# Hybrid trunk on one core: attention between projections, two convolution tiles by stacked taps on TensorE, the scan's carried part at full width

## The chip, the core and the metric

The kernel is one launch on one NeuronCore of a Trainium2 chip. The metric is the device time of a launch in microseconds (us), given as a median over runs. The core has four compute engines that work side by side, each through its own list of instructions in a fixed order: TensorE (PE: matmuls and transposes), VectorE (DVE: elementwise work), ScalarE (ACT: functions, copies) and GpSimd (POOL). SyncE (SP) issues the DMA transfers. The operands lie in SBUF (128 partitions); TensorE writes its sums to PSUM, which has 8 banks of 128 x 512 fp32. An engine that reaches an instruction whose inputs or whose buffer are not ready waits there, and all that stands behind it on that engine waits too.

## What is computed

Two layers over 576 tokens (512 of a prompt, 64 of eight samples with state). Layer 0 is a Conformer convolution (width 31, 512 channels) and sliding-window attention side by side, then a convolutional FFN; layer 1 is a Mamba-2 (SSD) mixer, then another FFN. The parts of the reference that the change touches:

```python
# layer 0, mixer
a_val, a_gate, q, k, v = split(h @ w_in)
u = a_val * sigmoid(a_gate)
padded = concatenate([conv_hist, u])                 # 30 rows of history ahead
c = silu(layernorm(causal_dwconv(padded, conv_w, conv_b)))   # 31 taps a channel
q, k = rope(rmsnorm(q)), rope(rmsnorm(k))
o = sink_attention(q, k, v, ...)                     # 8 heads, blocks of 128 queries, 256 keys
out = concatenate([c, o]) @ w_out

# layer 1, chunks of L = 128 tokens
w_intra = (cb[..., None] * decay * dtc[:, :, None])
y_diag = einsum('bclsgr,bcsgrp->bclgrp', w_intra, xc)
h_prev = ...                                         # state carried into each chunk
y_off = einsum('bclgn,bcgrpn,bclgr->bclgrp', cc, h_prev, exp(acum))
y = y_diag + y_off
```

## The kernel before

**Projections.** Everything lies with channels on the partitions and the 576 tokens along the free axis, in two halves of 288. Each projection takes weight tiles of 512 KB (`wr`, three buffers, loaded through SP's queue), splits them into a high part on ACT (`wh`, L148) and a low part on DVE (`wl`, L149), and does three matmuls a tile of 128 channels (`mm3`, L158 to L160: high x high, high x low, low x high). `units` runs a list of such projections, each with a function that empties its PSUM sums. `out_proj` adds the sums to the residual `x` on DVE (L257).

**Buffers and order.** SBUF is cut into slots; `S(name)` takes the slot that has been free longest, `free` gives it back, and whoever takes a slot waits for its last users. PSUM banks are dealt out in rings by name (`self.rings`): in this stage `mm` has banks 0 and 1, `sc` (attention scores) 4 to 6, `pt` (transposes) 7 and 2, `po` (attention sums) 3. A scheduler that runs at build time puts each engine's instructions into a fixed order from the program text, the dependencies and its own estimates.

**mix0.** The convolution input `u` of tile i (4 tiles of 128 channels) is written to `cap[i]` (prompt, 30 columns of history ahead) and `cas_v[i]` (samples) by the `val` units. The gate and value units of tiles 0 and 2 come first, then q, k and v, then tiles 1 and 3. The outputs `ca[i]` of the convolution take their slots at the start, with the gates. Tiles 0, 2 and 3 are convolved on DVE: ACT copies `cap` into overlapping segments (`seg`, L397), then one multiply (L686) and 30 multiply-adds (L688) run over 128 x 576. Tile 1 (`PC`) is convolved on TensorE (`pe_conv`): for each of the 31 taps ACT builds three diagonal matrices (L522 twice, L528), and TensorE does three float32r matmuls over 512 prompt columns (L524 to L526) and one fp32 matmul over 64 sample columns (L529). The pieces of `pe_conv` stand in the program between the four attention blocks, which come after all projections but `val` 1 and 3. Per block: scores (L581), softmax (maximum on DVE L553, exponential on ACT L560, scaling on DVE L564), transposes (L596) with a copy by ACT (L598), and the sums with the values (L601). The sample attention (L638 to L660) follows. After this come the layer norm of the convolution (`pm`, L696, needs all four `ca`) and two output projections of 192 matmuls each: of the attention (`oh`, `ol`), then of the convolution (`ch`, `cl`).

**The scan in mix1.** For each of 4 groups of 8 heads, `decays(r)` loads a row of cumulated decays broadcast to 128 partitions (`acb`, L955), makes the decay matrix of a head in `ew` (Relu L960 four times, Exp L961, product L962), and for chunks 1 to 3 scales C by the decay from the chunk's start (Exp L963, product L964). `outputs(t, pair)` takes two heads: 8 matmuls of the inner part (L979) and 6 of the carried part (L977, state times the scaled C) fill one bank `yp`, each with 64 columns of weights; L981 adds it to the skip term. There are 16 such blocks, which stand between the projection matmuls of the following group.

Of the kernel before, what the change touches and what calls it, by code (L numbers as in the profile page):

```python
# [6 lines left out]
F32 = mybir.dt.float32  # L7
# [18 lines left out]
for _name, _w in (  # L26
# [3 lines left out]
    ("cc_w", 24 * 4), ("cc_b", 24), ("dsk", 16), ("gn", 16),  # L30
# [8 lines left out]
for _name, _w in (  # L39
    ("ident", 128), ("prot", 128), ("blk2", 2), ("amask", 256), ("smask", 2 * 192),  # L40
    ("tri", 128), ("tris", 64), ("bmat", 64), ("bsel", 8), ("selx", 256), ("selm", 128),
    ("sel3", 192), ("bsel3", 4),
):
    CV[_name] = _n
    _n += _w
# [3 lines left out]
class Builder:  # L49
    NSLOT = 50  # L50
    EXTRA = 8
# [298 lines left out]
    def mix0(self):  # L350
# [49 lines left out]
        def a_val(i):  # L400
            def go(half, p):
# [3 lines left out]
                else:  # L405
# [89 lines left out]
        for i in (0, 2):  # L495
            sg[i], cap[i], ca[i] = self.S("sg"), self.S("cap", 542), self.S("ca")
# [6 lines left out]
        self.units([gate_unit(2), val_unit(2)] + qkv, 1)  # L503
        self.free(kg, ksq, krs, vf, cos, sin)
        for i in (1, 3):
            sg[i], cap[i], ca[i] = self.S("sg"), self.S("cap", 542), self.S("ca")
        self.units([gate_unit(1), gate_unit(3)], 1)

        self.rings = {"mm": [0, 1], "aux": [4, 5, 6, 7], "sc": [4, 5, 6], "pt": [7, 2], "po": [3]}
        pconv = {}  # L510

        def pe_conv(k0, k1):

            i = PC
            if not pconv:
                pconv[0] = self.pm(), self.pm()
            pp, ps = pconv[0]
            for k in range(k0, k1):
                dg = []
                for w in (cwh, cwl):  # L520
                    dg.append(self.segp.tile([P, P], F32R, tag="dg", bufs=4, name="dg"))
                    nc.scalar.activation(dg[-1], self.ident, AF.Copy, scale=w.bitcast(F32)[:, k:k + 1])  # L522
                sl = slice(k, k + NP)
                nc.tensor.matmul(pp, dg[0], cph[0][:, sl], start=k == 0, stop=False)  # L524
                nc.tensor.matmul(pp, dg[0], cph[1][:, sl], start=False, stop=False)
                nc.tensor.matmul(pp, dg[1], cph[0][:, sl], start=False, stop=k == 30)  # L526
                df = self.segp.tile([P, P], F32, tag="df", bufs=2, name="df")
                nc.scalar.activation(df, self.ident, AF.Copy, scale=self.pv("ca_w", i * 31 + k))  # L528
                nc.tensor.matmul(bt(ps[:, 0:64]), df, cas_v[i][:, :, k:k + 8], start=k == 0, stop=k == 30)  # L529
# [13 lines left out]
        of = [self.S("of") for _ in range(4)]  # L543
# [41 lines left out]
        def values(n, probs):  # L585
# [20 lines left out]
            self.free(held)  # L606
            for j in range(4):
                nc.scalar.activation(of[j][:, n * P:(n + 1) * P], po[:, j * P:(j + 1) * P], AF.Copy)

        ready = []  # L610
        for n in range(4):
            ready.append((n, scores(n)))
            if n == 0:
                self.units([val_unit(1), val_unit(3)], 1)
                self.norm_end()
            else:
                pe_conv((n - 1) * 31 // 4, n * 31 // 4)
            if len(ready) > 1:
                values(*ready.pop(0))
        pe_conv(3 * 31 // 4, 31)  # L620
# [651 lines left out]
```

## Time and profile before

| what | value |
|---|---|
| time, median of 3 runs | 1611.56 us (1610.28 to 1612.52) |
| the profiled execution's own time | 1613.28 us |
| its span (first to last instruction) | 1611.5 us |
| mean granted TensorE clock | 0.994 |
| TensorE busy | 1580.2 us, 98% of the span |
| DVE, ACT, POOL busy | 64%, 43%, 7% |
| first matmul of the `oh` projection | 187.70 us |
| first matmul of FFN 0 | 245.09 us |

How to read the lines that follow: a group's row gives line, engine, operation, tiles as output<-inputs, sizes, the count, then busy time in us, mean ns of one, and how long the engine sat idle ahead of them and for whom. A fp32 matmul shows as two records. The ends of matmuls are modelled, so where the pace matters the starts are compared. A row of the timeline gives the start, the time from the first start to the last end, and the count. A row of windows gives for each engine its busy time and, in brackets, how many instructions began; `PEclk` is the granted clock as a share of the full one.

### The profile page before, as it was taken

The numbers are of one execution on the slowest core, as the hardware profiler recorded it, in microseconds if no ns is written. First come the engines' busy times: TensorE is split into PE (matmuls) and PEld (weight loads), VectorE is DVE, ScalarE is ACT, GpSimd is POOL, SyncE is SP. The second block draws the span as 40 slices with busy tenths as digits, with TensorE's granted clock in tenths as the row PEclk, the third lists the DMA queues.
The fourth block names the chain that finished last, engine by engine and source line by source line (L and its number), as shares of the span: only waits on it lengthen the run. The fifth ranks groups of instructions, "written<-read, shape, count | busy, mean of one in ns | idle before, by whom it ended". The sixth has DMA issues, their size and how long they took to land.

```text
span 1611.5 us, 28699 instructions
## 1 busy us (share of the span) xinstructions
PE 1580.2 (98%) x11704; PEld 1502.4 (93%) x11704; DVE 1024.4 (64%) x1817; ACT 696.1 (43%) x1323; POOL 110.3 (7%) x322
## 2 busy tenths in 40 slices
PE   8999999999999999999999999999899999999999
PEld 8996899999999999998987997998799999999999
DVE  7898777664465364678795676676776653564552
ACT  7248853231222122478764656557452221221220
POOL 0000001000000000111202101101111000000000
PEclk9998999999999999999999999999999999999999
DMA  7222022222222222225235225224222222222222
GB/s 229 71 60 69 14 79 92 91 79 80 91 78 81 93 76 77 74 81 163 96 102 183 80 76 164 97 89 153 98 74 86 91 79 81 91 71 87 92 82 75
DMA packets 63632, 150.05 MB, mean 93 GB/s; under 512 B 18558, under 2 KB 19582, under 8 KB 63502
## 3 DMA queue, kind: packets, MB, share of 16 engines
q1 hardware_dynamic: 63502, 148.23, 29.6%
q8 instruction: 92, 1.51, 0.4%
q14 instruction: 38, 0.31, 0.1%
HBM read 133.86 MB, written 14.34 MB: 92 GB/s over the span
## 4 chain that ended last, share of the span: by engine, by line
PE 88%; DVE 5%; ACT 4%; DMA 3%; issue 1%; POOL 0%; SPq 0%; ACTq 0%; DVEq 0%; POOLq 0%
PE mm L158 26%; PE mm L160 25%; PE mm L159 25%; DMA acb<-acd 2%; PE yp L979 1%; DVE cconv L739 1%; PE pst L928 1%; PE pt L180 1%; ACT wh L148 1%; PE yp L977 1%; PE mm L524 1%; PE pyo L992 1%; PE pr L191 1%; PE pt L915 1%; PE mm L526 1%
## 5 line engine op out<-in xcount | busy, mean ns | idle before, releaser
L158 PE MATMUL mm<-hh,wh 128*128 128x288 f32 (+1 forms) x2288 | 681.0, 298 | 8.5 <-ACT wh L148 7.8
L160 PE MATMUL mm<-hh,wl 128*128 128x288 f32 x2288 | 679.6, 297 | 0.0
L159 PE MATMUL mm<-hl,wh 128*128 128x288 f32 (+1 forms) x2288 | 677.7, 296 | 0.0
L148 ACT ACTIVATE wh<-wr 128x1024 fp32r<-128x1024 f32 (+1 forms) x215 | 223.5, 1039 | 544.9 <-issue 284.8
L158 PEld LDWEIGHTS mm<-hh,wh 128*128 128x128 f32 (+1 forms) x2288 | 429.8, 188 | 14.7 <-ACT wh L148 8.0
L160 PEld LDWEIGHTS mm<-hh,wl 128*128 128x128 f32 x2288 | 429.6, 188 | 4.6 <-issue 2.8
L159 PEld LDWEIGHTS mm<-hl,wh 128*128 128x128 f32 (+1 forms) x2288 | 430.4, 188 | 3.5 <-issue 1.4
L149 DVE TENSOR_TENSOR wl<-wr,wh 128x1024 fp32r<-128x1024 f32 (+1 forms) x215 | 257.6, 1198 | 78.1 <-ACT wh L148 77.9
L158 PE MATMUL mm<-yh,wh 128*128 128x288 f32 x960 | 287.0, 300 | 3.6 <-ACT yh L168 2.5
L159 PE MATMUL mm<-yl,wh 128*128 128x288 f32 x960 | 287.5, 300 | 0.2 <-DVE yl L169 0.2
L160 PE MATMUL mm<-yh,wl 128*128 128x288 f32 x960 | 285.7, 298 | 0.0
L158 PEld LDWEIGHTS mm<-yh,wh 128*128 128x128 f32 x960 | 181.8, 190 | 8.4 <-issue 3.4
L159 PEld LDWEIGHTS mm<-yl,wh 128*128 128x128 f32 x960 | 182.0, 190 | 4.6 <-issue 3.2
L257 DVE TENSOR_TENSOR x<-x,mm 128x288 f32<-128x288 f32 x192 | 85.7, 452 | 155.7 <-PE mm L160 155.4
L160 PEld LDWEIGHTS mm<-yh,wl 128*128 128x128 f32 x960 | 181.8, 189 | 2.9 <-issue 2.8
L302 DVE TENSOR_TENSOR gbuf<-mm,rs 128x224 f32<-128x224 f32 x44 | 17.2, 392 | 107.7 <-PE mm L160 107.7
L313 ACT ACTIVATE gsilu<-gconv,par 128x512 f32<-128x512 f32 x44 | 31.9, 725 | 115.1 <-DVE gconv L310 115.0
L310 DVE SCALAR_TENSOR_TENSOR gconv<-gbuf,par,gconv 128x592 f32<-128x592 f32 x88 | 73.2, 832 | 1.5
L323 DVE TENSOR_TENSOR gsilu<-mm,gsilu 128x288 f32<-128x288 f32 x88 | 40.1, 455 | 49.9 <-PE mm L160 49.9
L688 DVE SCALAR_TENSOR_TENSOR ca<-seg,par,ca 128x576 f32<-128x576 f32 x90 | 71.3, 814 | 0.6
L739 DVE SCALAR_TENSOR_TENSOR cconv<-cbuf,par,cconv 128x600 f32<-128x600 f32 x72 | 61.5, 857 | 11.4 <-ACT cconv L737 10.3
L960 ACT ACTIVATE ew<-acb,ac 128x128 f32<-128x128 f32 x128 | 41.2, 391 | 45.2 <-DMA acb<-acd 34.5
(315 smaller groups left out, 1721.1 us busy)
## 6 DMA issues: line engine op xcount, KB each, us to landing
wr<-in_w_gate SPq DMA_DIRECT2D x44, 512.0 KB, 3.3
wr<-in_w_up SPq DMA_DIRECT2D x44, 512.0 KB, 3.4
wr<-in_w_in_o SPq DMA_DIRECT2D x40, 512.0 KB, 3.5
wr<-in_w_down SPq DMA_DIRECT2D x32, 448.0 KB, 3.4
wr<-in_w_down SPq DMA_DIRECT2D x16, 512.0 KB, 3.5
acb<-acd SPq DMA_DIRECT2D x32, 256.0 KB, 3.6
h<-in_h SPq DMA_DIRECT2D x32, 256.0 KB, 3.0
out_ssm_s<-h SPq DMA_DIRECT2D x32, 256.0 KB, 3.1
```

The source lines that it names most:

```text
L148: nc.scalar.activation(hi[:, :n], raw[:, :n], AF.Copy)
L149: nc.vector.tensor_tensor(lo[:, :n], raw[:, :n], hi[:, :n].bitcast(F32), op=SUB)
L158: nc.tensor.matmul(out, hi[:, ws], xh[:, sl], start=i == 0, stop=False)
L159: nc.tensor.matmul(out, hi[:, ws], xl[:, sl], start=False, stop=False)
L160: nc.tensor.matmul(out, lo[:, ws], xh[:, sl], start=False, stop=i == n - 1)
L257: nc.vector.tensor_tensor(self.x[m][:, sl], self.x[m][:, sl], p[:, :HB], op=ADD)
L310: nc.vector.scalar_tensor_tensor(cv[:, :592], g[:, k:592 + k], w(k), cv[:, :592], op0=MUL, op1=ADD)
L313: nc.scalar.activation(sl[:, :NP], cv[:, :NP], AF.Silu, bias=b)
L323: nc.vector.tensor_tensor(sl[:, HALF[half]], p[:, :HB], sl[:, HALF[half]], op=MUL)
L688: nc.vector.scalar_tensor_tensor(a, sv[:, :, k:k + 8], w, a, op0=MUL, op1=ADD)
L739: nc.vector.scalar_tensor_tensor(cv[:, :600], g[:, k:600 + k], w(k), cv[:, :600], op0=MUL, op1=ADD)
L960: nc.scalar.activation(ew[:, cs], acb[:, cs], AF.Relu, bias=ac[:, o:o + 1], scale=-1.0)
```

## The change

1. **Order in mix0.** The four blocks of attention now stand between the remaining projections: q, k, v directly after tile 0; then scores 0, gate and value 2, scores 1, values 0, gate and value 1, scores 2, values 1, gate and value 3, scores 3, values 2, the sample scores, tile 1's convolution, values 3, the sample values, tile 3's convolution.
2. **Two convolution tiles on TensorE, four taps at a time.** Tiles 1 and 3 (`PC = (1, 3)`) go through a copy in DRAM (`cad`), from which 32 transfers a tile read 32 channels each, shifted by 0 to 3 columns, so that the 128 rows hold 32 channels x 4 taps (`xp4` prompt, `xs4` samples). A weight of 128 x 32 (`w4`, built on POOL) then does four taps at once for 32 channels, in fp32: 8 steps x 4 column groups for the prompt (L536) and as many for the samples (L543). The diagonal matrices on ACT and the split of `cap` go. `ca[i]` takes its slot only when a tile is convolved. DVE keeps tiles 0 and 2.
3. **The carried part of the scan at full width.** `carried(t)` does state times unscaled C for two heads at once, one 128 x 128 x 128 matmul a chunk (L1014, three a block), and scales the product on DVE by `ea2`, the decays of both heads (two loads of 64 x 384, one Exp). `outputs` keeps the 8 matmuls of the inner part (L1027), adds the carried part in a separate DVE instruction, and `ew` is made in place in `acb`.

Lines move by some numbers: L158 to L160 become L160 to L162, L688 becomes L730, L564 L585, L581 L602, L596 L617, L601 L622, L696 L738.

On VectorE, before, the convolution's multiply-adds (L688) stand among the evacuations of the projections (`sg`, `cap`, `kg`) from early in mix0 on:

```order
L686 TENSOR_SCALAR ca<-seg,par 128x576
L382 TENSOR_TENSOR sg<-sg,rs 128x288
L380 TENSOR_TENSOR sg<-mm,rs 128x288
L688 SCALAR_TENSOR_TENSOR ca<-seg,par,ca 128x576
L382 TENSOR_TENSOR sg<-sg,rs 128x288
L149 TENSOR_TENSOR wl<-wr,wh 128x1024
L404 TENSOR_TENSOR cap<-mm,sg 128x288
L688 SCALAR_TENSOR_TENSOR ca<-seg,par,ca 128x576 x3
```

On VectorE, now, at the end of the attention (L585 is the last scaling of the sample softmax, L547 and L548 empty the banks of a convolution tile from TensorE, L171 splits the attention's output):

```order
L585 TENSOR_SCALAR sm<-sm,den 128x192 x2
L728 TENSOR_SCALAR ca<-seg,par 128x576
L730 SCALAR_TENSOR_TENSOR ca<-seg,par,ca 128x576
L547 TENSOR_SCALAR ca<-mm,par 128x512
L730 SCALAR_TENSOR_TENSOR ca<-seg,par,ca 128x576
L548 TENSOR_SCALAR ca<-mm,par 128x64
L730 SCALAR_TENSOR_TENSOR ca<-seg,par,ca 128x576
L728 TENSOR_SCALAR ca<-seg,par 128x576
L730 SCALAR_TENSOR_TENSOR ca<-seg,par,ca 128x576 x8
L171 TENSOR_TENSOR ol<-of,oh 128x576 x4
L730 SCALAR_TENSOR_TENSOR ca<-seg,par,ca 128x576 x35
L547 TENSOR_SCALAR ca<-mm,par 128x512
```

All 62 convolution instructions of tiles 0 and 2 (before: 93 of three tiles, spread over the stage) now stand behind the last softmax. The slot of tile 0's `ca` is one that tile 1's `xp4` gives back, so the first of them also waits for tile 1's matmuls; 14 more, with five additions to `x` (L259) between them, stand behind the rows shown.

On SyncE, before, behind the last value unit (`kct` and `vc` are the sample caches):

```order
L408 DMA out_ca_p<-cap 128x30
L409 DMA out_ca_s<-cas 1024x1x30
L284 DMA fhist<-in_ffn_hist 128x352
L626 DMA kct<-in_kct 128x512
L627 DMA vc<-in_vc 128x512
```

On SyncE, now, at the same place (`cad` is the copy in DRAM; the first two rows are the last of tile 1's 32 loads, which alternate in this way):

```order
L527 DMA xp_1320<-cad_203 32x536
L528 DMA xs_1322<-cad_203 32x8x32
L410 DMA out_ca_p<-cap 128x30
L411 DMA out_ca_s<-cas 1024x1x30
L414 DMA cad_204<-cap 128x542
L415 DMA cad_204<-cas 128x304
L640 DMA kct<-in_kct 128x512
L641 DMA vc<-in_vc 128x512
```

The sample caches now stand behind 32 small loads, which stand behind the last of the four weight tiles of the attention's output projection; another 32 loads for tile 3 follow the caches, ahead of the weights of the convolution's output projection.

On TensorE, one block of the scan before (`hst` is the carried state), and one now:

```order
L979 MATMUL yp<-ew,xdt 64x128 x4
L977 MATMUL yp<-acb,hst 64x128 x2
L979 MATMUL yp<-ew,xdt 64x128 x2
L977 MATMUL yp<-acb,hst 64x128 x2
L979 MATMUL yp<-ew,xdt 64x128 x2
L977 MATMUL yp<-acb,hst 64x128 x2
```

```order
L1014 MATMUL py<-cfm,hst 128x128 x3
L1027 MATMUL yp<-acb,xdt 64x128 x8
```

Fourteen matmuls of 64 weight columns became eight of 64 and three of 128; in most blocks projection matmuls stand between the two rows.

The diff, cut to its core:

```diff
-    NSLOT = 50
-    EXTRA = 8
+    NSLOT = 48
+    EXTRA = 10
...
                 if half == 0:
+                    sg[i], cap[i] = self.S("sg"), self.S("cap", 542)
...
-        PC = 1
-        cph = self.S("cph", 542, F32R), self.S("cpl", 542, F32R)
-        cwh, cwl = (self.segp.tile([P, 31], F32R, name=n_) for n_ in ("cwh", "cwl"))
-        self.split(self.pv("ca_w", PC * 31, 31), (cwh, cwl), slice(0, 31))
+        PC = (1, 3)
+
+        cad = {i: self.dp.tile([P, 846], F32, name=f"cad{i}") for i in PC}
...
-                    if i == PC:
-                        self.split(cap[i], cph, slice(0, 542))
+                    if i in PC:
+                        nc.sync.dma_start(cad[i][:, 0:542], cap[i])
+                        nc.sync.dma_start(cad[i][:, 542:846].rearrange("p (b c) -> p b c", c=38), cas_v[i])
                     else:
                         segment(i)
+                    self.free(cap.pop(i))
...
-        for i in (0, 2):
-            sg[i], cap[i], ca[i] = self.S("sg"), self.S("cap", 542), self.S("ca")
...
-        self.units([gate_unit(2), val_unit(2)] + qkv, 1)
+        self.units(qkv, 1)
...
+        def pe_conv(i):
+            xp4 = [self.S("xp4", 540) for _ in range(4)]
+            xsp = [self.S("xs4", 576) for _ in range(2)]
...
+            for c in range(4):
+                for j in range(4):
+                    n = 540 if j < 3 else 536
+                    m = 36 if j < 3 else 32
+                    r, rc = slice(j * 32, j * 32 + 32), slice(c * 32, c * 32 + 32)
+                    nc.sync.dma_start(xp4[c][r, 0:n], src[rc, j:j + n])
+                    nc.sync.dma_start(xs4[c][r, :, 0:m],
+                                      src[rc, 542:846].rearrange("p (b t) -> p b t", t=38)[:, :, j:j + m])
+            yield
+            pp, ps = self.pm(), self.pm()
+            for s in range(8):
+                k = slice(0, P if s < 7 else 96)
+                for c in (3, 2, 1, 0):
+                    w = w4[i][k, (s * 4 + c) * 32:(s * 4 + c) * 32 + 32]
+                    m = nc.tensor.matmul(pp[c * 32:c * 32 + 32, :], w, xp4[c][k, 4 * s:4 * s + NP], start=s == 0, stop=s == 7)
...
+            ca[i] = self.S("ca")
+            nc.vector.tensor_scalar(ca[i][:, :NP], pp, self.pv("ca_b", i), None, op0=ADD)
+            nc.vector.tensor_scalar(ca[i][:, NP:], ps[:, 0:64], self.pv("ca_b", i), None, op0=ADD)
+            self.free(xp4, xsp)
+            yield
...
+        p0 = scores(0)
+        self.units([gate_unit(2), val_unit(2)], 1)
+        p1 = scores(1)
+        values(0, p0)
+        self.units([gate_unit(1), val_unit(1)], 1)
+        p2 = scores(2)
+        values(1, p1)
+        convs = [pe_conv(i) for i in PC]
+        next(convs[0])
+        self.units([gate_unit(3), val_unit(3)], 1)
+        self.norm_end()
+        p3 = scores(3)
+        sample_loads()
+        next(convs[1])
+        values(2, p2)
+        sample_scores()
+        for _ in convs[0]:
+            pass
+        values(3, p3)
+        sample_values()
+        for _ in convs[1]:
+            pass
...
             sv = segs[i]
+            ca[i] = self.S("ca")
...
-                ew = self.S("ew", NP)
...
-                nc.scalar.activation(acb[:, P:NP], acb[:, P:NP], AF.Exp)
-                nc.vector.tensor_tensor(acb[:, P:NP], acb[:, P:NP], cf[:, P:NP], op=MUL)
-                return acb, ew
...
+            def carried(t):
+
+                ea2 = self.S("ea2", NP - P)
+                for hh in range(2):
+                    nc.sync.dma_start(ea2[hh * 64:hh * 64 + 64, :], acd[8 * g + 2 * t + hh, P:NP].partition_broadcast(64))
+                nc.scalar.activation(ea2, ea2, AF.Exp)
+                py = self.ps("py")
+                for c in range(1, 4):
+                    nc.tensor.matmul(py[:, (c - 1) * P:c * P], H[c - 1][:, t * P:(t + 1) * P], cf[:, c * P:(c + 1) * P],
+                                     start=True, stop=True)
+                nc.vector.tensor_tensor(ea2, ea2, py[:, 0:NP - P], op=MUL)
+                return ea2
...
+                    for hh in (1, 0):
+                        r = 2 * t + hh
+                        rows, ch = slice(hh * 64, hh * 64 + 64), slice(r * 64, r * 64 + 64)
+                        m = nc.tensor.matmul(yp[rows, cs], xdt[c][:, ch], pair[hh][:, cs], start=True, stop=True)
...
+                nc.vector.tensor_tensor(x[:, P:], x[:, P:], ea2, op=ADD)
```

More of the change, by code (lines that the diff above doesn't have):

```diff
@@ L1 @@
+import itertools
 import numpy as np
@@ L512, in pe_conv @@
[L512 to L529, printed above, removed]
+        w4 = {}
@@ L664, in mix0 @@
-        po_v = po[:, 0:256].rearrange("p (b j t) -> p b j t", j=4, t=8)
-        for j in range(4):
-            nc.scalar.activation(bt(of[j][:, NP:]), po_v[:, :, j, :], AF.Copy)
+                    nc.tensor.matmul(p[kv][:, P:192], qs[rows, bh * P:(bh + 1) * P], kf[rows, NP:], start=True, stop=True)
+                c0 = 32 + bh * 2
+                probs.append(softmax([p[kv][:, 0:192] for kv in range(2)], self.cv("smask", bh * 192, 192), rsq[:, c0:c0 + 2],
+                                     self.pv("sink_s", 0, 2), nsink[:, 8:10], 192, (0, 1)))
@@ L706, in mix0 @@
         self.out_proj([d["w_out_e"][1, c] for c in range(4)], oh, 4)
-        self.free(oh, list(ca.values()), list(cap.values()), cas, lrs, csq, *cph)
+        self.free(oh, list(ca.values()), cas, lrs, csq)
         self.norm_begin("norm_f0", True)
@@ L1145, in constants @@
     put("prot", prot)
+    put("m32", np.tile(np.eye(32, dtype=f), (4, 1)))
     half = np.arange(P) // 64
```

157 lines of the change are left out of this document (81 added, 76 removed).

## The prediction

> **What bounds the kernel now.** I read the page's busy shares first, then the chain that ended last, then windows of 10 us over mix0, then the timeline at its seams.
>
> ```profile
> PE 1580.2 (98%) x11704; PEld 1502.4 (93%) x11704; DVE 1024.4 (64%) x1817; ACT 696.1 (43%) x1323; POOL 110.3 (7%) x322
> PE 88%; DVE 5%; ACT 4%; DMA 3%; issue 1%; POOL 0%; SPq 0%; ACTq 0%; DVEq 0%; POOLq 0%
> 120.00:130.00 10.00, 9.99 (x56) 7.73 (x55) 9.63 (x34) 9.92 (x34) 0.00 (x0) 1.00 0.47 143
> 140.00:150.00 10.00, 10.00 (x47) 7.70 (x41) 4.94 (x14) 5.99 (x18) 0.00 (x0) 0.66 0.00 0
> 150.00:160.00 10.00, 7.85 (x42) 4.56 (x40) 8.72 (x27) 8.78 (x29) 0.00 (x0) 0.86 0.37 105
> ```
>
> TensorE bounds the kernel: 98% busy, 88% of the chain. So work taken off DVE or ACT gains nothing unless TensorE was waiting for it, and what counts in each stage is when its last matmul can start. In the windows of mix0 the second pair of numbers is TensorE, the third to last column the granted clock. Even in this stage, where DVE and ACT are over 90% busy at 120 to 130 us, TensorE is nearly full; it loses in 140 to 160, by a clock of 0.66 and 0.86 and some idle time.
>
> **mix0, what TensorE saves.** Tile 1's convolution now, and what would replace it:
>
> ```profile
> 119.31 0.50 PE L524 MATMUL mm<-cph,dg 128*128 128x512 f32 x1
> 120.25 0.47 PE L524 MATMUL mm<-cph,dg 128*128 128x512 f32 x1
> 754.83 1.07 PE L992 MATMUL pyo<-h,cfm 128*32 128x512 f32 x8
> 755.82 0.50 PE L999 MATMUL pst<-x,b 96*128 96x512 f32 x1
> ```
>
> One tap takes 120.25 - 119.31 = 0.94 us, 31 taps 29 us. The nearest row to the new matmuls is the scan's `pyo`: four column groups of 32 with 512 columns, fp32, eight records in 755.82 - 754.83 = 0.99 us; four one after the other would be four times as much per group, so the groups run side by side. Eight such steps are 7.9 us for the prompt; the samples (64 columns) I put at 0.15 a step, 1.2 us, from the 0.33 us that two records of 64 columns end to end take below as an upper end. That is 9 us a tile (8 to 11), 18 for both: 11 us less TensorE work. This is only worth something if TensorE is what the stage ends on.
>
> **mix0, when it ends.** Now these rows:
>
> ```profile
> 116.16 3.23 PE L581 MATMUL sc<-kf,qf 64*128 64x256 f32 x16
> 121.96 0.33 PE L529 MATMUL mm<-cas,df 128*128 128x64 f32 x2
> 179.71 0.87 PE L596 MATMUL pt<-ident,sm 128*128 128x128 f32 x6
> 181.32 1.08 PE L601 MATMUL po<-ptb,vt 128*64 128x512 f32 x4
> 180.01 0.82 DVE L688 SCALAR_TENSOR_TENSOR ca<-seg,par,ca 128x576 f32<-128x576 f32 x1
> 206.07 0.82 DVE L169 TENSOR_TENSOR cl<-ca,ch 128x288 fp32r<-128x288 f32 x2
> 186.37 1.70 PE L696 MATMUL pm<-ca,o 128*128 128x288 f32 x6
> 187.70 0.51 PE L158 MATMUL mm<-oh,wh 128*128 128x288 f32 x1
> 218.22 0.29 PE L158 MATMUL mm<-ch,wh 128*128 128x288 f32 x1
> 245.09 0.30 PE L158 MATMUL mm<-hh,wh 128*128 128x288 f32 x1
> ```
>
> The last input projection ends at 116.16, with block 0's scores already done; the DVE convolution ends at 180.8, and 7 us later the attention's output projection starts, whose 192 matmuls (187.70 to 218.22) cover the layer norm. The convolution's projection follows without a gap and ends at 245.09. Seen from DVE the before kernel is well laid: its 93 convolution instructions are done before they are wanted.
>
> In the changed kernel I count from U, the end of the last input projection. Three blocks' attention now lies ahead of it: scores 1 and 2, 2 x 3.2 = 6.4; 24 transposes at about 0.13 = 3.1; three `po` pairs, 3 x 1.05 = 3.1. U = 116.2 + 12.6 = 128.8, say 129.5 with small waits (up to 131).
>
> From U on, the order of DVE decides, shown above: the softmax of block 3, that of the samples, and only then all 62 convolution instructions. Their durations:
>
> ```profile
> L560 ACT ACTIVATE sm<-sm,neg,rsq 128x256 f32<-128x256 f32 (+2 forms) x36 | 20.1, 565 | 0.0
> L553 DVE CUSTOM_DVE_ANT_0 sm<-sc,cst 128x256 f32<-128x256 f32 (+2 forms) x36 | 12.0, 380 | 7.5 <-PE po L601 6.3 <-PE sc L581 1.1
> L564 DVE TENSOR_SCALAR sm<-sm,den 128x256 f32<-128x256 f32 (+2 forms) x36 | 9.3, 330 | 0.0
> L182 ACT ACT_TABLE_LOAD x3 | 3.8, 1283 | 0.1
> 122.36 3.00 DVE L688 SCALAR_TENSOR_TENSOR ca<-seg,par,ca 128x576 f32<-128x576 f32 x4
> 163.23 11.92 DVE L688 SCALAR_TENSOR_TENSOR ca<-seg,par,ca 128x576 f32<-128x576 f32 x14
> 186.79 2.76 DVE L169 TENSOR_TENSOR ol<-of,oh 128x576 fp32r<-128x576 f32 x4 [1.54 <-ACT oh L168]
> L678 DVE TENSOR_SCALAR ca<-mm,par 128x512 f32<-128x512 f32 x1 | 0.8, 751 | 1.8 <-PE mm L526 1.8
> L257 DVE TENSOR_TENSOR x<-x,mm 128x288 f32<-128x288 f32 x31 | 13.7, 450 | 7.6 <-PE mm L160 7.5
> ```
>
> Block 3: scores 3.3, the maxima hidden behind them but for about 1 us, a table load 1.3, eight exponentials at 0.57 = 4.5, scaling 8 x 0.33 = 2.6: about U+13. Samples: maxima 2 x 0.4, exponentials 2 x 0.6, scaling, and this again for the second half, with a hand-over of 0.2 to 1 us between engines at each of some eight changes: about U+22. Tile 1's convolution (9 us of TensorE, from U+13) ends at about the same time, and the first DVE instruction also waits for it. I take U+23 (U+20 to U+27).
>
> Then DVE works through: four in 3.00 us is (3.00 - 0.82)/3 = 0.73 apart where two tiles alternate, and fourteen in 11.92 is (11.92 - 0.82)/13 = 0.85 apart where one tile runs alone. Both tiles alternate in the new order, so 62 x 0.73 = 45; to this come the emptying of the banks of tiles 1 and 3 (0.75 for 512 columns, less for 64: 2), `ol` 2.8, five additions to `x` at 0.45, less what overlaps at the seams: 51 us (at 0.85: 58). The last convolution instruction ends at T = 129.5 + 23 + 51 = 203.5, against 180.8 before.
>
> What can TensorE do meanwhile? The attention's output projection needs PSUM banks, and each is given back by an addition that stands behind 47 of the 62 instructions, or by the emptying of tile 3's banks, which does too. That comes at U + 23 + 47 x 0.73 + 2.8 + 1 = U+61. Until then TensorE has the rest of the attention, tile 3's convolution and the output tiles that fit in the free banks; in its order these are 82 of the 192 matmuls ahead of the ones that wait for T, so from about U+48 on it mostly waits. The 110 left, at (218.22 - 187.70)/192 = 0.16 with the norm's small matmuls among them, and the eight `pm` matmuls are 1.7 + 17.6 = 19 to 21 us, which is as long as the norm needs (from the last `pm` at 186.4 to the last `cl` at 206.9 before). Then the convolution's projection, 245.09 - 218.22 = 26.9. FFN 0 starts at T + 21 + 26.9 = 251.4, or some 2 us later for the latencies at the start of the chain. Against 245.09 that is **+8 us** (0 with the short ends, +15 with the long ones). A change that empties TensorE by 11 us makes this stage longer, because it puts the convolution of DVE behind the softmax.
>
> There is also the clock:
>
> ```profile
> 157.47 0.80 PE L524 MATMUL mm<-cph,dg 128*128 128x512 f32 x1 [2.07 <-ACT dg L522]
> ```
>
> After 2.07 us of waiting that matmul took 0.80 instead of 0.47. The waits of the new stage are longer; I add **+1 us** (0 to 4) for slow matmuls after T and at tile 1's convolution. The Trainium skill (TensorE: Matmul & The Clock Gate, Part 1: The HAM clock gate) says that TensorE falls to half its clock after an idle window of about 3.4 us and needs about as long of work to leave it. The row above, with 2.07 us, shows that a gap shorter than that window is enough here. By the page, the one long wait before T would cost half of 3.4, some 1.7 us (an estimate), which would put the sum 0.7 higher.
>
> **The scan.** One block now, from a stretch without waits, and the row nearest to the new `py`:
>
> ```profile
> 764.13 0.66 PE L979 MATMUL yp<-ew,xdt 128*64 128x128 f32 x8
> 764.61 0.39 PE L977 MATMUL yp<-acb,hst 128*64 128x128 f32 x4
> 765.80 0.40 PE L158 MATMUL mm<-hh,wh 128*128 128x288 f32 x1
> 729.97 1.07 PE L902 MATMUL pc<-cfm,bfm 128*128 128x128 f32 x8
> L979 PE MATMUL yp<-ew,xdt 128*64 128x128 f32 x256 | 30.9, 286 | 6.6 <-DVE ew L962 6.5
> L977 PE MATMUL yp<-acb,hst 128*64 128x128 f32 x192 | 24.5, 281 | 2.0 <-DVE acb L964 2.0
> ACT ew L960 <- DMA acb<-acd: 34.5, 9, 10.0
> ```
>
> Fourteen matmuls take 765.80 - 764.13 = 1.67 us. The eight that stay take (764.61 - 764.13)/8 x 16 = 0.96; three of 128 columns, at (1.07 - 0.28)/7 = 0.11 a record, 0.68. Sum 1.64: the matmuls themselves gain nothing. What can be gained are the waits: 6.6 + 2.0 = 8.6 us idle, and slow matmuls behind them. Two Exp and two products of 384 columns a block become one Exp, one product and one addition, `py` waits for no decays, and the second head's wait falls ahead of the block. I take **-6 us**; the ends are -9 (all the idle time) and +4, when the 32 new loads of `ea2` or the longer queue delay `acb`, for which ACT already waits 34.5 us in nine places, up to 10.0 at once.
>
> **Sum.** +8 + 1 - 6 = +3. On the profiled execution's own 1613.28 that is 1616.3; that execution lies 1.7 above the median of 1611.56, so the forecast is **1614.6**.
>
> **The rivals.** About 0.2%, 3.2 us, is what a measurement of this kernel can tell from no change.
> - *Forecast*, late DVE convolution +5 to +12 and scan -3 to -8: about 1609 to 1618. Chance 0.45 (faster 0.03, same 0.25, slower 0.17). For it: the order of DVE is fixed. Against it: the start of the chain is a sum of small latencies.
> - *Faster*: TensorE finds its 11 us after all, because softmax and convolution overlap closely (start at U+20, 0 in mix0), and the scan's waits go: -7 to -9, about 1603. Chance 0.24. For it: the DVE stage of 51 us is covered for half by work that TensorE still has; against it: the PSUM banks.
> - *Slower by the scan*: a block waits just as long, since its decays come through the same chain (load, four Relu, Exp, product): +9 and 0 to +2, about 1622. Chance 0.20.
> - *Slower by the loads*: this one decides if the queue of SP becomes the bound.
>
> ```profile
> 109.25 0.33 SPq L139 DMA_DIRECT2D wr<-in_w_out_e  x1
> 110.32 0.34 SPq L408 DMA_DIRECT2D out_ca_p<-cap  x1
> 110.71 0.54 SPq L409 DMA_DIRECT2D out_ca_s<-cas  x1
> out_ca_s<-cas SPq DMA_DIRECT2D x4, 120.0 KB, 6.1
> ```
>
> One issue takes 0.34, a scattered one 0.54, so 32 loads take 14 us. They stand behind a weight tile that was issued at 109 before, some 7 us ahead of U; the caches then come at U+10 and land in time. If each load waits for the one eight places ahead, at the 6.1 us that the scattered one takes to land, it is 24 us, the sample scores start at U+20, the DVE chain at U+32: +18 in mix0, about 1626. Chance 0.08.
> - *The change does not do what it says*: the column groups run one after the other, four times 7.9 us a tile, and DVE's chain starts 20 us later: about 1635. Chance 0.03; the `pyo` row speaks against it.
>
> Slower is 0.17 + 0.20 + 0.08 + 0.03 = 0.48, same 0.25, faster 0.27. The range: up to 1627 it holds all but the last case; down to 1602 it holds most of the faster one.
>
> **What would show it.** Right, if the last convolution instruction (L730) ends near 203 and FFN 0's first matmul starts near 253; if TensorE idles some 15 to 25 us in mix0 with DVE as the releaser; and if idle time ahead of L1027 falls to 1 to 4 us. Wrong, if L730 starts before the last softmax ends, if TensorE is idle for a DMA ahead of the sample scores, or if L1027 idles as long as L979 did.

## The result, and the profile after

| kernel | median | ratio of the runs to the kernel before's, 95% interval | FFN 0's first matmul in the profile |
|---|---|---|---|
| before | 1610.92 us (4 runs) | 1 | 245.09 |
| changed | 1621.70 us (1620.26 to 1625.76, 4 runs) | 1.0073 [1.0049, 1.0098] | 259.93 |

The change costs 10.8 us. The forecast was 1614.6 with a range of 1602 to 1627: the time is slower, as the largest chance had it, and inside the range, but above the forecast case's own 1609 to 1618. The busy shares of the changed kernel's page:

```profile
PE 1561.5 (96%) x11709; PEld 1484.8 (92%) x11709; DVE 1006.2 (62%) x1786; ACT 659.4 (41%) x1211; POOL 112.9 (7%) x324
```

TensorE has 19 us less to do than before (1580.2) and the kernel is still longer, so it waits more. Where, the windows of mix0 show (the second pair of numbers is TensorE, the fourth DVE, the third to last column the granted clock):

```profile
140.00:150.00 10.00, 4.52 (x20) 1.11 (x20) 2.56 (x10) 7.42 (x24) 0.00 (x0) 0.78 0.87 159
180.00:190.00 10.00, 2.63 (x82) 1.31 (x72) 10.00 (x15) 0.00 (x0) 0.00 (x0) 0.83 0.01 2
190.00:200.00 10.00, 1.39 (x6) 1.39 (x7) 10.00 (x15) 0.00 (x0) 0.00 (x0) 0.50 0.00 0
200.00:210.00 10.00, 9.67 (x53) 9.03 (x53) 10.00 (x18) 1.06 (x1) 0.00 (x0) 0.82 0.00 0
```

From 182 to 198 us TensorE has nothing to do while DVE is full. TensorE's waits (engine, line and tile, for whom, us in total, times, longest) and the seams of the stage on its timeline:

```profile
PE mm L160 <- DVE ca L547: 16.0, 1, 16.0
PE po L622 <- ACT ptb L619: 6.0, 3, 5.5
PE mm L161 <- DVE hl L360: 2.7, 2, 1.4
```

```profile
134.13 0.49 PE L602 MATMUL sc<-kf,qf 64*128 64x256 f32 x2
174.65 7.08 PE L536 MATMUL mm<-xp,w 128*32 128x512 f32 x64
181.55 1.08 PE L543 MATMUL mm<-xs,w 128*32 128x64 f32 x64
198.62 0.61 PE L160 MATMUL mm<-oh,wh 128*128 128x288 f32 x1 [15.99 <-DVE ca L547]
203.75 0.30 PE L160 MATMUL mm<-oh,wh 128*128 128x288 f32 x1
233.05 0.30 PE L160 MATMUL mm<-ch,wh 128*128 128x288 f32 x1
259.93 0.30 PE L160 MATMUL mm<-hh,wh 128*128 128x288 f32 x1
```

The last input projection ends at 134.13, FFN 0 starts at 259.93. Between 198.62 and 203.75 TensorE issues 21 matmuls, 0.24 apart; from then on they are 0.13 apart. After 16 us of waiting it goes at half its pace for about 5 us, which costs 5.1 - 21 x 0.133 = 2.3 us. DVE in the same stage:

```profile
159.36 0.58 DVE L728 TENSOR_SCALAR ca<-seg,par 128x576 f32<-128x576 f32 x1 [0.18 <-PE mm L536]
163.51 5.92 DVE L730 SCALAR_TENSOR_TENSOR ca<-seg,par,ca 128x576 f32<-128x576 f32 x8
197.81 0.75 DVE L547 TENSOR_SCALAR ca<-mm,par 128x512 f32<-128x512 f32 x1
209.97 0.81 DVE L730 SCALAR_TENSOR_TENSOR ca<-seg,par,ca 128x576 f32<-128x576 f32 x1
```

The 62 convolution instructions start at 159.36, released by tile 1's last matmul, run (5.92 - 0.82)/7 = 0.73 apart, and end at 210.8; L547, for which TensorE waits, stands behind all but the last 14 of them. In the scan (groups of the changed kernel over mix1, and the two parts of a block on its timeline, each with the projection matmul behind it):

```profile
L1027 PE MATMUL yp<-acb,xdt 128*64 128x128 f32 x256 | 19.7, 297 | 6.5 <-DVE acb L1003 6.5
L1014 PE MATMUL py<-cfm,hst 128*128 128x128 f32 x96 | 13.8, 282 | 0.1
878.04 0.83 PE L1014 MATMUL py<-cfm,hst 128*128 128x128 f32 x6
878.62 0.38 PE L160 MATMUL mm<-hh,wh 128*128 128x288 f32 x1
882.65 1.09 PE L1027 MATMUL yp<-acb,xdt 128*64 128x128 f32 x16
883.67 0.40 PE L162 MATMUL mm<-hh,wl 128*128 128x288 f32 x1
```

A block's matmuls take 0.58 + 1.02 = 1.60 us, against 1.67 before in a block that is not split. The wait of 2.0 ahead of the carried part is gone, the 6.5 ahead of the inner part is still there.

One caution on single profiles. The profiled execution of before had the clock at 0.66 and 0.86 in 140 to 160 us. Three runs below with the same instructions in the same order up to there (e2, e8, e11) reach FFN 0 at 241.97, 241.93 and 241.96, so 3.1 of its 245.09 belong to this one execution. Where sizes count, the medians over several rounds decide.

### The profile page after: what moved, and what is told of

Read it like the earlier page. It is cut to its first block, busy times and chain, and to the rows that moved or that the text cites. A ratio compares the mean times of both kernels' runs of the same rounds, so it can differ in the third digit from the quotient of the medians.

```text
span 1618.5 us, 28690 instructions
## 1 busy us (share of the span) xinstructions
PE 1561.5 (96%) x11709; PEld 1484.8 (92%) x11709; DVE 1006.2 (62%) x1786; ACT 659.4 (41%) x1211; POOL 112.9 (7%) x324
## 4 chain that ended last, share of the span: by engine, by line
PE 44%; DMA 3%; DVE 3%; ACT 2%; issue 1%; SPq 0%; ACTq 0%; DVEq 0%
PE mm L162 13%; PE mm L161 13%; PE mm L160 13%; DMA acb<-acd 1%; DVE cconv L781 1%; PE yp L1027 1%; DMA h<-in_h 1%; PE pyo L1044 1%; DMA out_ssm_p<-hst 1%; PE ysp L1080 0%; PE pt L957 0%; ACT acb L1001 0%; ACT wh L150 0%; DMA out_ssm_s<-h 0%; PE pst L970 0%
## 5 line engine op out<-in xcount | busy, mean ns | idle before, releaser
L160 PE MATMUL mm<-hh,wh 128*128 128x288 f32 (+1 forms) x2288 | 682.6, 299 | 8.6 <-ACT wh L150 8.0
L162 PE MATMUL mm<-hh,wl 128*128 128x288 f32 x2288 | 682.8, 299 | 0.0
L160 PEld LDWEIGHTS mm<-hh,wh 128*128 128x128 f32 (+1 forms) x2288 | 432.4, 189 | 13.3 <-ACT wh L150 8.2
L162 PEld LDWEIGHTS mm<-hh,wl 128*128 128x128 f32 x2288 | 432.1, 189 | 4.6 <-issue 2.9
L160 PE MATMUL mm<-yh,wh 128*128 128x288 f32 x960 | 285.7, 299 | 0.7 <-DVE x L259 0.5
L162 PE MATMUL mm<-yh,wl 128*128 128x288 f32 x960 | 284.5, 297 | 0.0
L162 PEld LDWEIGHTS mm<-yh,wl 128*128 128x128 f32 x960 | 181.2, 189 | 4.3 <-issue 2.4
L160 PEld LDWEIGHTS mm<-yh,wh 128*128 128x128 f32 x960 | 181.1, 189 | 2.7 <-DVE x L259 1.1
L259 DVE TENSOR_TENSOR x<-x,mm 128x288 f32<-128x288 f32 x192 | 85.5, 451 | 152.3 <-PE mm L162 152.1
L1001 ACT ACTIVATE acb<-acb,ac 128x128 f32<-128x128 f32 x128 | 41.3, 390 | 34.5 <-DMA acb<-acd 30.2
L318 DVE TENSOR_TENSOR gsilu<-gsilu,rs 128x576 f32<-128x576 f32 x44 | 33.3, 758 | 26.7 <-ACT gsilu L316 26.7
```

The costliest lines, as they stand in the source:

```text
L160: nc.tensor.matmul(out, hi[:, ws], xh[:, sl], start=i == 0, stop=False)
L162: nc.tensor.matmul(out, lo[:, ws], xh[:, sl], start=False, stop=i == n - 1)
L259: nc.vector.tensor_tensor(self.x[m][:, sl], self.x[m][:, sl], p[:, :HB], op=ADD)
L318: nc.vector.tensor_tensor(sl, sl, rs, op=MUL)
L1001: nc.scalar.activation(acb[:, cs], acb[:, cs], AF.Relu, bias=ac[:, o:o + 1], scale=-1.0)
```

## The experiments

Theory: in mix0 the whole DVE convolution has moved behind the softmax and TensorE waits for it; the scan gains. The rivals: TensorE lacks PSUM banks, or the loads, or what POOL disturbs; the new order itself costs; the scan gains only because a block's matmuls stand together. Each kernel was timed beside the kernel before on the same chip (medians 1606.8 to 1608.7). The last column is from one execution each, which can lie several us from the median: those of e1 and e2 lie 4.6 and 5.2 us below, those of e6 and e7 3.3 and 5.5 above.

| run | median, us | ratio, 95% interval | FFN 0 |
|---|---|---|---|
| e1_early_ca | 1604.28 | 0.9972 [0.9954, 0.9991] | 240.56 |
| e2_scan_alone | 1600.07 | 0.9944 [0.9925, 0.9963] | 241.97 |
| e3_mix0_alone | 1628.00 | 1.0125 [1.0096, 1.0154] | 263.60 |
| e4_bank_by_act | 1626.14 | 1.0106 [1.0079, 1.0133] | 266.95 |
| e5_caches_first | 1600.31 | 0.9957 [0.9942, 0.9972] | 240.13 |
| e6_taps_late | 1605.34 | 0.9977 [0.9964, 0.9990] | 245.09 |
| e7_both | 1599.90 | 0.9947 [0.9926, 0.9967] | 246.44 |
| e8_scan_whole_blocks | 1606.15 | 0.9992 [0.9980, 1.0005] | 241.93 |
| e9_order_alone | 1601.55 | 0.9952 [0.9934, 0.9970] | 242.89 |
| e10_old_order_stacked | 1604.89 | 0.9979 [0.9964, 0.9994] | 247.11 |
| e11_scan_loose | 1600.60 | 0.9953 [0.9935, 0.9972] | 241.96 |
| e12_stacked_tiles_first | 1597.90 | 0.9929 [0.9908, 0.9949] | 238.46 |

### The two halves of the change, apart

`e2_scan_alone` is the kernel before with the change's `decays`, `carried` and `outputs`; `e3_mix0_alone` is the changed kernel with the scan of before.

> The kernel before with the scan's part of the change alone. Theory A (the carried part at full width saves some 10 us whatever mix0 does): mix1 (first projection matmul of mix1 to the first of FFN 1) takes 505 to 509 us instead of 517, time 1599 to 1603. Rival B (the gain came from another phase of waits after the longer mix0): mix1 takes 513 or more, time 1607 to 1611.

> The changed kernel with the scan of the kernel before. If the parts add up: FFN 0 starts at 258 to 262 us, mix1 takes 515 to 519, time 1628 to 1633. If they don't (the longer mix0 itself shortened the scan): time 1620 to 1624.

The scan alone is worth 0.56% of 1608, 9.0 us (6 to 12); the new mix0 alone costs 1.25%, 20 us (15 to 25). Their sum, +11, is what the whole change costs, so an effect of the halves on each other is not seen within these intervals. Both times came as expected; in their profiles e2's mix1 was shorter than expected (500.6) and e3's FFN 0 started later (263.60).

### The slot of `ca` is what puts the convolution behind the softmax

`e1_early_ca` changes only when the two outputs of the DVE convolution take their slots:

```diff
+        for i in (0, 2):
+            ca[i] = self.S("ca")
         self.units([gate_unit(0), val_unit(0)], 2, first)
...
             sv = segs[i]
-            ca[i] = self.S("ca")
```

> The changed kernel, but the outputs ca of tiles 0 and 2 take their slots at the start of mix0, so that DVE's multiply-adds can stand among the projections again. Theory A (mix0 became longer because the DVE convolution stands behind the last softmax): the 62 instructions are done before the attention's end, the 16.0 us wait of TensorE for ca L547 goes, FFN 0 starts at 233 to 242 us instead of 259.9, time 1596 to 1604. Rival B (the chain of small latencies from the last projection through softmax, small loads and sample scores sets the end): DVE is free earlier, but FFN 0 still starts after 250, time 1612 or more.

DVE's last convolution instructions, FFN 0's start, and the longest wait of TensorE in the stage:

```profile
144.80 3.38 DVE L731 SCALAR_TENSOR_TENSOR ca<-seg,par,ca 128x576 f32<-128x576 f32 x4
240.56 0.29 PE L160 MATMUL mm<-hh,wh 128*128 128x288 f32 x1
PE sc L656 <- DMA kct<-in_kct: 4.3, 1, 4.3
```

The convolution ends at 148.2 instead of 210.8, the wait of 16.0 is gone, and FFN 0 starts 19.4 us earlier; of the time, 1.0% (16 us) comes back. Only the time at which two slots are taken was changed, so the cause of most of the loss is shown. The next wait is one for the sample cache `kct`, which stands behind tile 1's 32 loads. What may keep e1 (0.9972) above e2 (0.9944) need not lie in mix0: in their profiles e1's mix0 ends 1.4 earlier, and its mix1 is 7.2 longer (507.8 against 500.6), 6.4 of this in waits. In mix1 TensorE waits 17.0 to 19.5 us in all eight kernels with the stacked tiles and the new scan, and 12.8 to 16.4 in the three with the new scan and the old convolutions (e2, e9, e11); why was not traced.

### The banks instead of DVE

In `e4_bank_by_act` ACT empties the banks of the stacked tiles, so that L547 no longer stands in DVE's list:

```diff
-            nc.vector.tensor_scalar(ca[i][:, :NP], pp, self.pv("ca_b", i), None, op0=ADD)
+            nc.scalar.activation(ca[i][:, :NP], pp, AF.Identity, bias=self.pv("ca_b", i))
...
```

(and the same for the samples' bank)

> The changed kernel, but ACT instead of DVE empties the PSUM banks of the two convolution tiles, so that the banks of tile 3 come free some 15 us earlier. Theory A (the end of DVE's list of multiply-adds sets the end; the wait for ca L547 is only where TensorE happens to stand): the wait at L547 goes or shrinks, TensorE then waits for the additions to x or for pm, FFN 0 starts at most 3 us earlier, time 1617 to 1622. Rival C (the banks are what holds the stage): FFN 0 starts 8 us or more earlier, time 1613 or less.

```profile
PE pm L738 <- DVE ca L730: 19.3, 1, 19.3
207.63 4.21 PE L738 MATMUL pm<-ca,o 128*128 128x288 f32 x8 [19.28 <-DVE ca L730]
```

The wait only changes its name: TensorE now waits 19.3 us at the layer norm, for the last convolution instructions, which end at 210.5, against 210.8 in the changed kernel. That TensorE waited for a bank said where it stood, not what it lacked. FFN 0 even starts 7.0 us later in this profile: 48 instead of 79 of the 192 matmuls of the attention's output projection are done when the convolution ends, so 31 more follow, at 0.16 each 5.0 us, and TensorE runs at half its pace until 212.6. Theory A expected 1617 to 1622; at 1626.14 the time is longer, though its interval overlaps the changed kernel's.

### What holds the stage after that

`e5_caches_first` is e1 with `sample_loads()` moved ahead of tile 1's loads. `e6_taps_late` is e1 with the stacked weights built later: POOL's product gets its taps from a DVE copy that waits for `k`.

```diff
...
+            wq = self.Z(f"wq{i}", 32, bufs=1)
+            nc.vector.scalar_tensor_tensor(wq, kf[:, 0:32], 0.0, self.pv("ca_wq", i * 32, 32), op0=MUL, op1=ADD)
...
```

`e7_both` has both.

> e1_early_ca with the sample caches kct and vc loaded ahead of tile 1's 32 small loads. Theory D (what is left of the loss in e1 is the wait of 4.3 us for kct behind the small loads, and the slow clock of tile 1's convolution behind it): the wait goes, FFN 0 starts 4 to 8 us earlier than in e1 (240.6), at 233 to 237 us, the time falls by 4 to 8 us against e1. Rival E (the small loads then come later and TensorE waits for xp4 instead): FFN 0 within 2 us of e1.

> e1_early_ca, with POOL's two products of 128 x 1024 (the stacked weights w4) held back until k is projected, by two small DVE instructions that read k times zero. Theory F (DVE stands still while POOL multiplies: two DVE instructions took 2.47 us instead of 0.82 and 0.75 at the start, and TensorE waited 2.8 us for hl): the slow pair moves with POOL to where TensorE does not wait, the wait for hl goes, time 2 to 3.5 us under e1. Rival G (the start is slow for another reason, such as the loads): the two slow instructions stay at 16 to 21 us.

> e1_early_ca with both: caches first and w4 late. If D and F hold and add up: FFN 0 starts at 230 to 235 us, time 6 to 11 us under e1, 1594 to 1599. If one hides the other, no better than the better of e5 and e6.

The longest wait of e5 in the stage:

```profile
PE sc L656 <- DVE mx L576: 4.5, 1, 4.5
```

The 4.3 us for the cache became 4.5 us for DVE's maxima, which give the scores their bank back; FFN 0 starts at 240.13 against 240.56, as rival E had it, but for another wait than E's. The times of e1 and e5 are not told apart. For e6, first the start of the changed kernel (POOL, then DVE), then e6 where its product runs:

```profile
15.93 4.46 POOL L513 TENSOR_TENSOR w<-cst,par 128x1024 f32<-128x1024 f32 x2 [14.73 <-DMA cst<-in_cst]
15.46 0.76 DVE L206 TENSOR_TENSOR ssq<-ssq,sq 128x576 f32<-128x576 f32 x1
16.13 2.48 DVE L360 SCALAR_TENSOR_TENSOR hl<-x,par,hh 128x576 fp32r<-128x576 f32 x1
18.53 2.47 DVE L206 TENSOR_TENSOR ssq<-ssq,sq 128x576 f32<-128x576 f32 x1
20.93 0.80 DVE L360 SCALAR_TENSOR_TENSOR hl<-x,par,hh 128x576 fp32r<-128x576 f32 x1
```

```profile
16.08 0.81 DVE L360 SCALAR_TENSOR_TENSOR hl<-x,par,hh 128x576 fp32r<-128x576 f32 x1
43.46 4.92 POOL L517 TENSOR_TENSOR w<-cst,wq 128x1024 f32<-128x1024 f32 x2 [42.26 <-DVE wq L516]
46.90 2.10 DVE L733 SCALAR_TENSOR_TENSOR ca<-seg,par,ca 128x576 f32<-128x576 f32 x1
PE pr L430 <- DVE qg L448: 2.4, 1, 2.4
PE pt L621 <- DVE sm L589: 6.6, 1, 6.6
```

While POOL builds the weights, two DVE instructions take 2.48 and 2.47 instead of 0.80 and 0.76, and TensorE waits 2.7 us for `hl`. With the product moved, the start is normal and a convolution instruction beside it takes 2.10: the slow pair goes where POOL goes. It gains nothing: in this profile TensorE waits elsewhere instead, 2.4 us shortly behind the moved product and 6.6 for the sample softmax. That these are the same delay is argued, not tried. e7 (0.9947) does not add the two up either; it is not told apart from e5 (0.9957).

### The old order, the old convolution

`e9_order_alone` has the new order and the new scan with before's convolution: tile 1 by 31 taps in three pieces, ahead of scores 3, values 2 and values 3, three tiles on DVE, all `ca` at the start. `e10_old_order_stacked` is e1 with before's order (gates 1 and 3 ahead of scores 0, both value units behind it).

> The kernel before with the new scan and the new order of mix0, but with the old convolutions (tile 1 by 31 taps on TensorE, three tiles on DVE, ca taken at the start). Theory J (the new order gains nothing by itself: behind the last input projection only one block's attention is left, so TensorE waits there for a chain of softmax steps that the old order hid under other blocks; the 31 taps now fill that wait): FFN 0 starts at 238 to 246 us, time within 4 us of e2_scan_alone (1600). Rival K (the order was worth its 12 us of attention moved under the projections): FFN 0 at 230 to 235, time 1588 to 1594.

> The new scan and both stacked convolution tiles, ca of tiles 0 and 2 taken at the start, but in the old order: all projections first, then the four blocks of attention with the two convolutions between them. Theory J (stacking is worth its 11 us of TensorE and 24 us of DVE where other work covers the loads and the softmax): FFN 0 starts at 228 to 236 us, time 1588 to 1596, under e2_scan_alone and under e5_caches_first. Rival L (the 64 small loads or the softmax chain hold this order as well): FFN 0 at 240 or later, time 1599 or more.

e9 is as fast as e2 (0.9952 and 0.9944): the order by itself gives and costs nothing that can be measured. In e10 (0.9979, FFN 0 at 247.11) the time that stacking saves TensorE does not show either, as rival L expected. Two rows of its stage, its longest wait and the start of tile 1's convolution:

```profile
PE sc L657 <- DVE mx L577: 6.4, 1, 6.4
163.29 1.07 PE L539 MATMUL mm<-xp,w 128*32 128x512 f32 x8
```

In the old order both value units come late, so that the stacked tiles' 64 loads and the softmax can lie on the path together. This is argued from the order: TensorE's named waits in this stage are for the maxima (6.4), copies of the softmax (3.5) and `hl` (2.3), none for a load, and the clock fell to 0.82 and 0.50 at 130 to 150 us.

### Why the scan gains

`e8_scan_whole_blocks` leaves the scan's arithmetic as before and only keeps a block's 14 matmuls together, second head first, as the change does. `e11_scan_loose` is e2 without that fixed order.

> The kernel before with one edit: in the scan the 14 matmuls of a block are kept together (second head first), as in the changed kernel, but they stay the same matmuls. Theory H (most of the scan's gain is that blocks are no longer split: before, in 13 of 16 the first two records ran alone among projection matmuls at 0.36 us, and the rest took 1.67 again): mix1 takes 511 to 514 us instead of 517, time 3 to 6 us under before. Rival I (the gain is in the work itself, 24.5 us of L977 against 13.8 of L1014 busy): mix1 within 2 us of before, and the waits for decays only move to the head of the block.

> e2_scan_alone without the rule that keeps a block's eight matmuls together, and with the first head first, so that blocks may be split as in the kernel before. Theory I (the gain is that of the full-width product and of the waits it saves): within 2 us of e2, 1598 to 1602. Theory H (it is the unsplit blocks): 3 to 6 us slower than e2, 1603 to 1606.

Whole blocks alone give 0.08%, with 0 in the interval and at most 0.2%, 3.2 us; without the fixed order the gain stays (0.9953). By the times, then, most of the gain is the product at full width with what comes with it (fewer instructions for the decays, `ew` made in place), and not the order within a block. e8's groups and e2's, over mix1:

```profile
L979 PE MATMUL yp<-ew,xdt 128*64 128x128 f32 x256 | 23.1, 279 | 5.9 <-DVE ew L962 5.9
L977 PE MATMUL yp<-acb,hst 128*64 128x128 f32 x192 | 19.2, 275 | 1.2 <-DVE acb L964 1.2
```

```profile
L985 PE MATMUL yp<-acb,xdt 128*64 128x128 f32 x256 | 18.2, 279 | 5.2 <-DVE acb L961 5.2
L972 PE MATMUL py<-cfm,hst 128*128 128x128 f32 x96 | 13.3, 276 | 0.1
```

The named waits account for 1.8 us of 9. The traces say more when mix1, from its first projection matmul to the first of FFN 1, is taken apart into TensorE's waits over 0.15 us, its slow clock (the share that was not granted, 0.010 before, times the span) and the rest, which is the matmuls themselves at full clock:

| kernel | scan | mix1, us | waits | slow clock | rest |
|---|---|---|---|---|---|
| before | before's | 517.1 | 18.0 | 5.1 | 494.0 |
| e3 | before's | 514.7 | 18.4 | 1.7 | 494.6 |
| e8 | before's, whole blocks | 510.4 | 20.3 | 1.7 | 488.4 |
| e11 | full width, loose | 505.0 | 13.5 | 3.4 | 488.0 |
| e2 | full width, whole blocks | 500.6 | 12.8 | 5.1 | 482.7 |
| changed | full width, whole blocks | 507.0 | 17.7 | 6.8 | 482.5 |

The rest repeats within 1.4 us: the other seven kernels with the new scan and the stacked tiles have 482.1 to 483.5. So in the changed kernel the scan's gain is not in the waits but in some 11.5 us less matmul time: 5.2 in the blocks' matmuls, 4.4 in the samples' product `pyo`, 2.3 in the projections (0.4 more in the others). Whole blocks and the full width bring about 6 each; before, 13 of the 16 blocks ran split, their first two records alone among projection matmuls. e8's mix1 fell below the 511 to 514 of theory H, but its time shows little of that (1.3, at most 3.2); 2.3 of its 6 are lost again to waits. What hides the remainder, and why `pyo` gets shorter, is open.

### A version with the stacked tiles first

`e12_stacked_tiles_first` is e1 with tile 1's gate and value ahead of q, k and v, its loads on POOL's queue, its convolution between values 0 and gate 2, tile 3's units ahead of tile 2's, and tile 2's `ca` taken only ahead of its gate.

```diff
-        self.units(qkv, 1)
+        self.units([gate_unit(1), val_unit(1)] + qkv, 1)
...
```

> The new scan and the new kinds of convolution, but tile 1's gate and value units stand directly behind tile 0's, and tile 3's ahead of tile 2's, so that the stacked tiles' small loads have 50 us and 20 us more before they are wanted; tile 1's loads go through POOL's queue, ca of tile 0 is taken at the start, tile 2's before its gate. Theory M (in e1, e5 and e10 it is the loads of xp4 behind the last projections and tile 3's convolution in the middle of the output projection that hold the stacked tiles back, not the stacking): both convolutions end before the attention does, FFN 0 starts at 222 to 234 us, time 1583 to 1594, under e2_scan_alone (1600). Rival N (the softmax chain behind the last projection, or POOL's and SP's issue of the loads, holds it in any order): FFN 0 at 238 or later, time 1597 or more.

```profile
150.00:160.00 10.00, 9.99 (x136) 4.36 (x136) 8.79 (x35) 9.99 (x35) 0.00 (x0) 1.00 0.44 155
238.46 0.29 PE L160 MATMUL mm<-hh,wh 128*128 128x288 f32 x1
```

Behind its first matmul TensorE now waits 4.4 us in mix0, 2.3 of them for `hl`, and FFN 0 starts at 238.46, 3.5 us ahead of e2. The stacked tiles take 11.6 us less of TensorE than e2's 31 taps (18.3 against 29.9, from start to start), but the other matmuls of the stage got 8 us longer: input projections 3.3 (2.3 of it the wait for `hl`), transposes 2.5, the attention's output projection 2.4; why was not traced. Start and time fall into rival N's ranges, but N's wait for the softmax chain is not there. At 0.9929 [0.9908, 0.9949] e12 beats both kernels, some 23 us below the changed one; against e2, 0.9944 [0.9925, 0.9963], it is not told apart.

## Why the prediction was right in sign and short in size

- **What bounds the kernel: right.** TensorE at 98% meant that only its own work and waits count, and the change turned 19 us of its work into waiting and more.
- **What stacking saves: right.** Predicted were 9 us a tile (8 to 11); tile 3 takes 181.55 - 174.65 = 6.9 and 1.1, in sum 8.0. The four column groups run side by side, so the rival that they don't is out.
- **DVE behind the softmax: right, and shown by e1.** The chain starts 25.2 after U (predicted 23), lasts 51.4 (51), at the predicted 0.73 an instruction, and FFN 0 starts 49.1 after T, the end of the last convolution instruction (48). The idle time has the predicted size (15 to 25 us; 16.0 for DVE and 6.0 for the attention's copies) and mostly the predicted releaser.
- **mix0's size: the step that failed.** The text put +8 and +1 for the clock; alone the stage costs +20 (15 to 25), and the profile has 259.93 - 241.95 = 18.0. The mis-sized term is the start, "U = 129.5": U came at 134.1. The attention ahead of it took its 12.5 us (12.6 in the sum). On top came 2.7 of waits for `hl` beside POOL's weight product, which the text did not price at all, 1.5 by which the input projections' matmuls were longer, 0.5 of waiting of the scores for maxima and 0.6 in small pieces, where the text had 0.7 for all small waits. Of the other differences, 3.1 lie in the base: the profiled 245.09 held a larger clock loss than three other executions of the same instructions. The start of the chain and its length took 2.7 more, the path from T to FFN 0 1.3. In sum 4.6 + 3.1 + 2.7 + 1.3 = 11.7 on top of the 251.4 - 245.09 = 6.3 that the count gave. The clock's +1, put after T, stands at 2.3 where TensorE resumes at 198.62; the DVE chain ends later than that, so what it can delay lies within the 1.3 from T to FFN 0. The Trainium skill (TensorE: Matmul & The Clock Gate, Part 1) would have given 1.7 (an estimate) by its 3.4 us; the slow stretch here is about 5 us.
- **The scan: sign right, size short, the reason wrong.** Predicted -6 (-9 to +4), measured -9.0 (-12 to -6). The text put the matmuls' own gain at nothing and the waits ahead of the blocks at all of it. In the changed kernel TensorE's waits in mix1 stayed (17.7 against 18.0), and ahead of L1027 they are 6.5, as ahead of L979 before, which the text had named as a sign of being wrong; the matmuls got some 11.5 us shorter. The step that failed is the sample: 1.67 is an unsplit block from a stretch without waits, while 13 of 16 were split, and `pyo` and the projections were not counted.
- **The range: in part luck.** The mix0 error of +11 and the scan's of -3 point opposite ways, and 1621.7 lies in the range through the width that other mechanisms had given it. The forecast case's 1609 to 1618 was also narrower than its terms: +12 and -3 on 1611.56 give 1620.6.
- **The rivals.** "Slower by the scan" named nearly the time that came, 1622, and was wrong in its mechanism: the scan gained and mix0 lost. "Slower by the loads" is out as the cause, since e1 gets 16 us back with all loads where they were; the load queue is only the next wait (4.3 us), and e5 shows another behind it. "Faster" needed softmax and convolution side by side: only e12 comes near that, with the loads and the convolution moved as well.

## What to carry to other kernels

Taking a buffer as late as possible can move a whole chain of work behind whatever gives that buffer back; where a queue of one engine ends a stage, look at when its output slots are taken before weighing the work itself. A wait's named releaser tells where an engine stands: give that buffer back by another route, and if the wait returns under another name, it was the chain behind it. Price a change of small matmuls over its whole stage and not from one block in a stretch without waits. And take a stage's base from several executions, since one profile can hold some us of clock that the next one doesn't.

## What the runs showed of the hardware

- POOL's 128x1024 product slows DVE instructions on two SBUF inputs that run beside it: 0.80 to 2.48 us and 0.76 to 2.47, and 0.81 to 2.10 for a convolution instruction when the product is moved (e6). The Trainium skill (SBUF — State Buffer, Who interferes with whom) states this: a DVE instruction with two inputs in SBUF contends with a GpSimd instruction that reads SBUF, through ports that one of them holds at a time. The trace agrees.
- After 16.0 us of waiting TensorE issued at half its pace for about 5 us. A fall also came without such a wait, and a wait of 2 us need not bring it. Four executions ran mix0 with the same instructions and a wait of 2.06 or 2.07 at the same place. Around that wait (150 to 160 us) the clock was 0.86 in before and 0.83 in e11, but 1.00 in e2 and e8; at 140 to 150 it was 0.66 in before and 0.83 in e8 with TensorE busy throughout. The prediction read the slow matmul behind that wait as its effect; as the wait was followed by a fall in two executions of four, these rows don't show that. e2's rows:

```profile
140.00:150.00 10.00, 9.87 (x61) 6.84 (x61) 6.58 (x24) 8.13 (x26) 0.00 (x0) 1.00 0.00 0
150.00:160.00 10.00, 7.86 (x48) 5.35 (x47) 10.00 (x31) 9.40 (x33) 0.00 (x0) 1.00 0.36 105
PE mm L524 <- ACT dg L522: 2.1, 1, 2.1
```
